# Layout of the on-chip pools at the change from FFN layer one to layer two: order of the pools, a ring of three row tiles, inner rows in the 2 KB ring

## The chip, the cores and the metric

The kernel runs on one core of a Trainium2 chip. Its engines work side by side, each through its own list of instructions in order: TensorE (PE: matmuls, with their weight loads as PEld), VectorE (DVE), ScalarE (ACT), GpSimd (POOL) and SyncE (SP), which issues nearly all DMA transfers here. They meet through semaphores. The metric is the device time in microseconds; lower is better. Data lies in HBM, in the on-chip SBUF (128 partitions; sizes below are bytes of one partition) and, for sums of matmuls, in PSUM banks.

## The reference, cut to what matters

One decoder block in float32: a mixing layer (pooling and stick-breaking attention), then a feed-forward layer, then a norm. The sequence has 2048 rows, the model width is 1024, the hidden width of the feed-forward layer is 4096.

```python
def reference(x, norm1_g, w_in, pool_w, pool_scale, pool_out_g, attn_out_g,
              w_out, norm2_g, w_up, w_down, final_g):
    B, S, _ = x.shape
    h = x
    for _ in range(DEPTH):
        hn = rmsnorm(h, norm1_g)
        proj = jnp.einsum('bsd,de->bse', hn, w_in)
        ...
        h = h + jnp.einsum('bse,ed->bsd', mixed, w_out)
        hn2 = rmsnorm(h, norm2_g)
        up = jnp.einsum('bsd,df->bsf', hn2, w_up)
        act = jnp.square(jax.nn.relu(up))
        h = h + jnp.einsum('bsf,fd->bsd', act, w_down)
    return rmsnorm(h, final_g)
```

The change concerns `up` (layer one of the feed-forward part), `act`, and the start of the product with `w_down` (layer two).

## The kernel before

**Arithmetic.** A float32 operand is split into two fp32r parts, high (ScalarE, L146) and low (VectorE, L147: operand minus high part). A product of two operands is three matmuls: high by high, high by low, low by high. Both layers are computed as a product of 2 x 2 blocks in Winograd's form, with seven products P1 to P7 in place of eight, of sums and differences of the blocks: for each half q of the sequence (1024 rows), A11, A12, A21, A22 are the blocks of the left operand (two halves of these rows by two halves of the inner width), S1 to S4 their sums.

**Layer one, `up()`.** `su` in HBM holds the row operands of layer one. For q = 0, then q = 1, the seven left operands are loaded through the ring `srp` (tiles `sr` of 4 KB, 4 slots, L929), split into `sa` (one pool of two tiles for each of the seven products: sap0 for P1, sap1 for P2, sap2 for P6, sap3 for P5, sap4 for P7, sap5 for P4, sap6 for P3) and kept for all 16 columns of that half. For a column m, 1 MB of `w_up` comes into `rb` (pool `rba` or `rbb`), its sums go to `rt` (pool `rtp`), and each product's weights are split into a tile `hw` of the pool `hlp`. A product is twelve matmuls of 128 x 512 (L1051) into a bank pX, pY or pZ; the products of one column follow each other as P2, P6, P5, P7, then P1 of the next column, P4, P3. After a product, `post()` takes the bank: ScalarE copies it (`p1`, `u2`, `u3`; L988), VectorE adds banks and copies (L996, L1004, L1020), ScalarE applies relu and square (L982, L983), and VectorE makes the sums s1, s2, s4 that layer two needs (L1011, L1014, L1016, L1024). These tiles have 2 KB each and come from the ring `avp` (11 slots); SP stores them to `sd` in HBM (L977).

**Inner sums.** For q = 1, columns come in pairs (m, m + 8). For A12 and A22 layer two uses a second level of the same form, and its row sums are made here, in the second column of each pair: `inner_rows(m)` loads two rows of q = 0 back from `sd` into one tile `hr` of 4 KB out of the ring `srp` for A22 and one for A12, both when P1 of the column is done (L870); `inner_sums` makes j1, j2 (from `avp`) and two sums in place in `hr` (L882 to L888), and stores the four to `sdi` (L880).

**Layer two, `down()`.** Steps of P1 (then P6, P7, ...): weights `wr` from `w_down` (L1120, pool `rt`) are split into `wd` (pool `t8`), rows `ar` from `sd` (L1170, pool `rs`) into `ad` (pool `s8`), and 24 matmuls for each q follow (L1391). For P1 a second `wr` is subtracted from the first (`minus`, L1124) and stored to `td` (L1126) for later use. `res` (L1195) are residual rows.

**What sets the order.** The kernel's source sets what is done; a scheduler orders the instructions of each engine when the program is built, knowing the pools and which memory comes free when. Pools are placed one behind another in the order in which they are opened, from the lowest free address. Those of layer two are opened after those of layer one have been closed, so they lie over them, and with `reuse_waits="tile"` a tile waits for exactly the earlier tiles that it overlaps. Where the pools of the two layers lie (first byte to end, in KB from the first byte of the stack that both share):

```
layer one: rtp 0-8, hlp 8-32, rba 32-40, srp 40-56 (four tiles of 4), sap0 to sap3 from 56 (16 each),
           sap6, pup, rbb, avp (11 of 2), sap4, sap5
layer two: rlp 0-16, tmp2 16-35, rs 35-55 (five of 4), rt 55-79 (six of 4), t8 (three of 8), s8 (five of 8),
           pup (eight of 8), rsp
```

So the first `rs` tiles lie over `rba` and `srp`, and the first `rt` tile over the last kilobyte of `srp` and over sap0. The last of the four `srp` slots holds the last `hr` tile.

All loads and stores named here go through SP in its one order, with at most eight on their way at a time: each new one takes one of eight semaphores in turn, and waits for the transfer that had it before.

Of the kernel before, what the change touches and what calls it, by code (L numbers as in the profile page):

```python
# [8 lines left out]
F32 = mybir.dt.float32  # L9
# [4 lines left out]
ALU = mybir.AluOpType  # L14

P = 128
S = 2048
D = 1024
T = 512
# [14 lines left out]
NEG = -1.0e30  # L34
RATIO_FRONT = (0.3, 0.4, 0.15, 0.4, 0.4, 0.3)
RATIO_TAIL = 0.6
SR = 4
LB = 4
UA = 4
LA = 5  # L40
DA = 2
# [5 lines left out]
def hymba_block(ctx: ExitStack, tc: tile.TileContext, xT, gains, w_in, pool_w, w_out, w_up, w_down, out):  # L47
    nc = tc.nc
    PS = bass.MemoryType.PSUM
# [86 lines left out]
    sd = [[[dram.tile([P, 2, T], F32, name=f"sd{q}_{i}_{c}") for c in range(8)] for i in range(7)] for q in range(2)]  # L136
# [701 lines left out]
    A11, A12, A22, S1, S2, S3, S4 = range(7)  # L838
# [19 lines left out]
    def up(pools, more):  # L858

        saps, hlp, rba, rtp, srp = pools  # L860
        NM = NF // 2
        cols = [(q, m + x * (NM // 2)) for q in range(2) for m in range(NM // 2) for x in range(2)]
        halves = {}

        def inner_rows(m):

            for i in (A22, A12):
                halves[i, 0] = r = srp.tile([P, 2, T], F32, tag="sr", name="hr")
                for x in range(2):
                    at = m + x * (NM // 2)  # L870
                    nc.sync.dma_start(r[:, x], sd[0][i][at // 2][:, at % 2])

        def inner_sums(m, i, t):

            if m < NM // 2:
                halves[i, 1] = t
                return
            a, r = halves.pop((i, 1)), halves.pop((i, 0))
            m -= NM // 2
            keep = lambda n, v: nc.sync.dma_start(sdi[i][n][m // 2][:, m % 2], v)  # L880
            s1, s2 = (avp.tile([P, T], F32, tag="av", name=n) for n in ("j1", "j2"))
            nc.vector.tensor_tensor(s1, a, t, ALU.add)  # L882
            keep(0, s1)
            nc.vector.tensor_tensor(s2, s1, r[:, 0], ALU.subtract)
            keep(1, s2)
            nc.vector.tensor_tensor(r[:, 0], r[:, 0], a, ALU.subtract)
            keep(2, r[:, 0])
            nc.vector.tensor_tensor(r[:, 1], r[:, 1], s2, ALU.subtract)  # L888
            keep(3, r[:, 1])

        what = {"P1": (A11, (0, 0), "Y", True, False), "P2": (A12, (0, 1), "X", True, True),
                "P6": (S2, (1, 1), "Y", False, False), "P5": (S1, (1, 0), "Z", True, False),
# [9 lines left out]
        raw, sums, ops, left_ops, ps, keep = {}, {}, {}, {}, {}, {}  # L902
# [67 lines left out]
        def post(q, m, s):  # L970
            k = keep.setdefault((q, m), {})
            x, y, z = (ps.get((q, m, b)) for b in "XYZ")
            new = lambda name: avp.tile([P, T], F32, tag="av", name=name)

            def put(i, t):
                if q == 0 or m >= NM // 2 or i not in (A12, A22):
                    nc.sync.dma_start(sd[q][i][m // 2][:, m % 2], t)  # L977
                if q and i in (A12, A22):
                    inner_sums(m, i, t)

            def act_of(i, src, t):
                nc.scalar.activation(t, src, AF.Relu)  # L982
                nc.scalar.activation(t, t, AF.Square)  # L983
                k[i] = t

            def copy(name):
                k[name] = pup.tile([P, T], F32, tag=name, name=name)
                nc.scalar.activation(k[name], y, AF.Copy)  # L988

            if s == "P1":  # L990
                copy("p1")
                if q and m >= NM // 2:
                    inner_rows(m - NM // 2)
            elif s == "P2":
                t = new("a11")
                nc.vector.tensor_tensor(t, x, k["p1"], ALU.add)  # L996
                act_of(A11, t, t)
                put(A11, t)
            elif s == "P6":
                copy("u2")  # L1000
            elif s == "P7":
                copy("u3")
                t = new("a22")
                nc.vector.tensor_tensor(t, z, k["u3"], ALU.add)  # L1004
                act_of(A22, t, t)
                put(A22, t)
            elif s == "P4":
                t = new("a21")
                act_of("A21", y, t)
                k[S1] = new("s1")  # L1010
                nc.vector.tensor_tensor(k[S1], t, k[A22], ALU.add)  # L1011
                put(S1, k[S1])
                k[S2] = new("s2")
                nc.vector.tensor_tensor(k[S2], k[S1], k[A11], ALU.subtract)  # L1014
                put(S2, k[S2])
                nc.vector.tensor_tensor(t, k[A11], t, ALU.subtract)  # L1016
                put(S3, t)
            elif s == "P3":
                t = new("a12")
                nc.vector.tensor_tensor(t, z, k["u2"], ALU.add)  # L1020
                act_of(A12, t, t)
                put(A12, t)
                s4 = new("s4")
                nc.vector.tensor_tensor(s4, t, k[S2], ALU.subtract)  # L1024
                put(S4, s4)
# [10 lines left out]
        rbb, pup, avp, psu = more()  # L1036
        load(*cols[1])
        lefts = [(g, q, s) for g, (q, m, s) in enumerate(slots) if m == 0 and not (q == 0 and s in order[:LB])]
        for g, (q, m, s) in enumerate(slots):
            while lefts and lefts[0][0] <= g + LA:  # L1040
                make_left(*lefts.pop(0)[1:])
            if q == 0 and 2 <= m < 6 and s in SUMS:
                sums_second(m - 2, SUMS.index(s))
            bank, first, last = what[s][2:]
            if first:
                ps[q, m, bank] = psu.tile([P, T], F32, tag=bank, name="p" + bank)
            t, w = ps[q, m, bank], ops.pop(g)
            for c in range(G):
                a = left_ops[q, s][c // 2]
                for x, (wx, ax) in enumerate(((0, 0), (0, 1), (1, 0))):  # L1050
                    nc.tensor.matmul(t, w[:, wx, c], a[:, ax, c % 2], start=first and c == 0 and x == 0,  # L1051
                                     stop=last and c == G - 1 and x == 2, skip_group_check=True)
            post(q, m, s)
            if g == 1:
                root_last(1, sslast, psu, "R")
            elif g in (6, 10):
                pr, i = psu.tile([P, T], F32, tag="R", name="pr"), g // 10
                spread(pr, yrlast[:, i])
                nc.scalar.activation(rlast[:, i], pr, AF.Copy)
            if g + UA < len(slots):  # L1060
                make_weights(g + UA)
                q2, m2, s2 = slots[g + UA]
                n = cols.index((q2, m2)) + 2
                if s2 == "P3" and n < 2 * NM:
                    load(*cols[n])

    def down(pools):
        t8, s8, rs, rt, pup, rsp, rlp, tmp_, psb = pools

        SPLIT = {"P4": A22, "P2": A12}  # L1070
        order = (("P1", A11), ("P6", S2), ("P7", S3), ("P4", A22), ("P5", S1), ("P2", A12))
# [109 lines left out]
        V = {}  # L1181
# [5 lines left out]

        def val(name, q):
            if (name, q) not in V:
                V[name, q] = pup.tile([P, 4, T], F32, tag="val", name=name)  # L1190
            return V[name, q]

        def add_residual(t, j, half, n):
# [231 lines left out]
    def catch_up(n):  # L1425
        for _ in range(n):
            with ExitStack() as behind:
                for ins in (last_split[0], done[0]):
                    if ins:
                        behind.enter_context(tc.issue_after(ins.ins))  # L1430
                later.pop(0)()
# [23 lines left out]
    def begin_ffn():  # L1455

        catch_up(len(later))
        for scope in (last_scope, out_scope, left_scope):
            scope.close()
        spool = lambda name, bufs, **kw: left_scope.enter_context(tc.tile_pool(name=name, bufs=bufs, reuse_waits="tile", **kw))  # L1460
        sap = {}
        rtp, hlp, rba, srp = (spool(n, b) for n, b in (("rtp", 1), ("hlp", UA + 2), ("rba", 1), ("srp", SR)))
        for i in range(LB):
            sap[i] = spool(f"sap{i}", 2)

        def more():
            sap[6], pup, rbb, avp = spool("sap6", 2), spool("pup", 2), spool("rbb", 1), spool("avp", 11)
            sap[4], sap[5] = (spool(f"sap{s}", 2) for s in (4, 5))
            return rbb, pup, avp, spool("psu", 2, space=PS)

        layer.append(up([sap, hlp, rba, rtp, srp], more))
        next(layer[0])

    def ffn():
        catch_up(len(later))
        front_scope.close()
        for _ in layer.pop():
            pass
        left_scope.close()
        with ExitStack() as scope:  # L1480
            spool = lambda name, bufs, **kw: scope.enter_context(tc.tile_pool(name=name, bufs=bufs, reuse_waits="tile", **kw))

            rlp, tmp2, rs, rt, t8 = spool("rlp", 2), spool("tmp2", 2), spool("rs", 5), spool("rt", 6), spool("t8", DA + 1)
            s8, pup, rsp = spool("s8", 2 * DA + 1), spool("pup", 8), spool("rsp", 2)
            down([t8, s8, rs, rt, pup, rsp, rlp, tmp2, spool("psb", 1, space=PS)])

    x0_scope = inner.enter_context(ExitStack())

# [19 lines left out]
    tail(True)  # L1508
    run()
    ffn()  # L1510


# [60 lines left out]
```

## Time and profile before

| what | value |
|---|---|
| median of 3 runs (1943.66, 1947.26, 1946.0) | 1946.0 us |
| the profiled execution, its own time | 1947.62 us |
| its span in the profile | 1945.7 us |
| mean granted TensorE clock | 0.991 |
| layer one, q = 1, and the turn to layer two | about 980 to 1328 us |

How to read what follows. The page and the views of the trace name an engine, a line of the kernel (L1051), what is written and read by the program's names (`pY<-sa,hw`), a count (x12) and times in microseconds. `SPq` is a transfer at the time of its issue by SP, `DMA` in the chain the transfer from issue to landing. In the view of waits a row names who waited, for whom, then the total, how often, and the longest. In the timeline a row is start, length, what, and in brackets how long the engine stood idle before it and what ended that. In windows a row is the stretch, its length, the busy time and count of TensorE's instructions where it is asked for TensorE (left out where it isn't), the granted clock (1.00 is full), the DMA engines' mean busy share (the packets' time can overlap to just over 1) and GB/s. In the list of DMA issues a row ends with KB and the median time from issue to landing.

### The profile page before, as it was taken

To read this page: it belongs to the slowest core of one execution; us is meant where nothing else is said; L and a number is where in the kernel's file an instruction comes from. 1 tells how busy PE (TensorE), PEld (TensorE's weight loads), DVE (VectorE), ACT (ScalarE), POOL (GpSimd) and SP (SyncE) were. 2 spreads that over 40 slices of the span, in tenths; PEclk is the share of its full clock that TensorE was granted. 3 is DMA by queue.
4 is the path that set the end of the run, shared out by engine and by line. 5 is a ranking of instruction groups with operands and counts; after the bars stand their busy time and mean duration, and the time that the engine had idled before them with its cause. 6 is when DMAs were issued, how large, how long until landed. Compare 5 with 4: busy or idle time off the path is not lost.

```text
span 1945.7 us, 26308 instructions
## 1 busy us (share of the span) xinstructions
PE 1905.2 (98%) x9043; PEld 1589.0 (82%) x9043; DVE 1384.6 (71%) x2026; ACT 994.7 (51%) x1580; POOL 206.3 (11%) x399
## 2 busy tenths in 40 slices
PE   9999999999999999999999999997999999999997
PEld 7888888887888888888878888875888888887887
DVE  6887799667876975777586777665565548649874
ACT  5565576455544555455575555553333255424643
POOL 0212123102111110000000000000020020006120
PEclk9999999999999999999999999998999999999999
DMA  6685787898696954677486666549898859957852
GB/s 222 205 271 178 232 273 215 253 325 272 235 381 231 336 188 145 221 245 251 171 265 220 222 217 239 203 166 388 301 343 303 293 203 317 335 191 267 320 205 89
DMA packets 197359, 483.44 MB, mean 248 GB/s; under 512 B 22496, under 2 KB 42976, under 8 KB 193120
## 3 DMA queue, kind: packets, MB, share of 16 engines
q1 hardware_dynamic: 197072, 481.40, 71.7%
q8 instruction: 73, 1.20, 0.3%
q14 instruction: 70, 0.57, 0.1%
q10 hardware_dynamic: 144, 0.26, 0.0%
HBM read 320.10 MB, written 161.48 MB: 248 GB/s over the span
## 4 chain that ended last, share of the span: by engine, by line
PE 72%; DVE 3%; DMA 1%; issue 1%; ACT 0%; POOL 0%; SPq 0%; DVEq 0%; ACTq 0%
PE pb L1391 21%; PE pY L1051 18%; PE pZ L1051 9%; PE pb L1229 7%; PE pX L1051 4%; PE pd L177 4%; PE pd L175 3%; PE pd L176 3%; PE pb L1334 1%; PE pr L228 1%; DVE ad L147 0%; DVE u L1200 0%; DMA sr<-su 0%; PE pm L202 0%; PE po L672 0%
## 5 line engine op out<-in xcount | busy, mean ns | idle before, releaser
L1391 PE MATMUL pb<-ad,wd 128*128 128x512 f32 x1872 | 429.6, 391 | 16.1 <-ACT ad L146 16.1
L1391 PEld LDWEIGHTS pb<-ad,wd 128*128 128x128 f32 x1872 | 352.6, 189 | 89.6 <-ACT ad L146 16.5
L1051 PE MATMUL pY<-sa,hw 128*128 128x512 f32 x1536 | 366.0, 390 | 2.5 <-ACT u L988 2.5
L1051 PEld LDWEIGHTS pY<-sa,hw 128*128 128x128 f32 x1536 | 289.0, 188 | 63.4 <-ACT u L988 3.3
L175 PE MATMUL pd<-h,hl 128*128 128x512 f32 x752 | 299.6, 398 | 0.7 <-DVE qkr L421 0.7
L177 PE MATMUL pd<-h,hl 128*128 128x512 f32 x752 | 296.9, 395 | 0.0
L176 PE MATMUL pd<-h,hl 128*128 128x512 f32 x752 | 296.4, 394 | 0.0
L147 DVE TENSOR_TENSOR ad<-ar,ad 128x1024 fp32r<-128x1024 f32 x136 | 175.6, 1300 | 50.5 <-ACT ad L146 50.2
L146 ACT ACTIVATE ad<-ar 128x1024 fp32r<-128x1024 f32 x136 | 142.5, 1051 | 115.3 <-PE pb L1391 69.1
L1051 PE MATMUL pZ<-sa,hw 128*128 128x512 f32 x768 | 184.9, 389 | 0.0
L1051 PEld LDWEIGHTS pZ<-sa,hw 128*128 128x128 f32 x768 | 144.4, 188 | 29.9
L175 PEld LDWEIGHTS pd<-h,hl 128*128 128x128 f32 x752 | 142.1, 189 | 28.2 <-DVE qkr L421 1.0
L177 PEld LDWEIGHTS pd<-h,hl 128*128 128x128 f32 x752 | 141.7, 188 | 27.8
L176 PEld LDWEIGHTS pd<-h,hl 128*128 128x128 f32 x752 | 141.9, 189 | 27.0
L146 ACT ACTIVATE hl<-raw 128x512 fp32r<-128x512 f32 x168 | 103.9, 630 | 107.1 <-PE pd L177 69.4
L1229 PE MATMUL pb<-ad,wd 128*128 128x512 f32 x672 | 154.3, 390 | 3.4 <-DVE ad L147 3.4
L1229 PEld LDWEIGHTS pb<-ad,wd 128*128 128x128 f32 x672 | 125.6, 188 | 31.8 <-DVE ad L147 5.9
L147 DVE TENSOR_TENSOR hl<-raw,hl 128x512 fp32r<-128x512 f32 x168 | 114.6, 687 | 51.1 <-ACT hl L146 48.1
L147 DVE TENSOR_TENSOR hw<-rt,hw 128x512 fp32r<-128x512 f32 x128 | 87.6, 687 | 72.8 <-ACT hw L146 72.7
L146 ACT ACTIVATE wd<-wr 128x1024 fp32r<-128x1024 f32 x48 | 50.9, 1060 | 147.4 <-PE pb L1391 111.6
L147 DVE TENSOR_TENSOR wd<-wr,wd 128x1024 fp32r<-128x1024 f32 x48 | 58.8, 1224 | 67.6 <-ACT wd L146 67.3
L1051 PE MATMUL pX<-sa,hw 128*128 128x512 f32 x384 | 93.0, 389 | 0.0
(213 smaller groups left out, 2628.5 us busy)
## 6 DMA issues: line engine op xcount, KB each, us to landing
ar<-sd SPq DMA_DIRECT2D x104, 512.0 KB, 5.6
rb<-in_w_up_dram SPq DMA_DIRECT2D x32, 1024.0 KB, 6.0
wr<-in_w_down_dram SPq DMA_DIRECT2D x64, 512.0 KB, 5.6
sd<-a SPq DMA_DIRECT2D x112, 256.0 KB, 3.4
raw<-in_w_in_dram SPq DMA_DIRECT2D x50, 512.0 KB, 4.9
sd<-s SPq DMA_DIRECT2D x96, 256.0 KB, 3.4
raw<-in_w_out_dram SPq DMA_DIRECT2D x32, 512.0 KB, 5.5
ar<-sdi SPq DMA_DIRECT2D x32, 512.0 KB, 5.1
```

The lines of the kernel that those rows point to most:

```text
L146: nc.scalar.activation(hi, src, AF.Copy)
L147: return nc.vector.tensor_tensor(lo, src, hi.bitcast(F32), ALU.subtract)
L175: nc.tensor.matmul(ps, hl[:, 0, c], hi, start=(k == 0), stop=False)
L176: nc.tensor.matmul(ps, hl[:, 0, c], lo, start=False, stop=False)
L177: mm = nc.tensor.matmul(ps, hl[:, 1, c], hi, start=False, stop=(k == n - 1))
L228: mm = nc.tensor.matmul(pr[:, b * P:(b + 1) * P], yr[:, x, b:b + 1].to_broadcast([P, P]), identr, start=(b == 0 and x == 0), stop=(b == TB ...
L1051: nc.tensor.matmul(t, w[:, wx, c], a[:, ax, c % 2], start=first and c == 0 and x == 0, stop=last and c == G - 1 and x == 2, skip_group_che ...
L1229: nc.tensor.matmul(b, t[:, wx, 2 * (kk % 2) + c, i * P:(i + 1) * P], a[:, ax, c], start=p in ("P1", "P5", "P2") and kk == 0 and c == 0 and ...
L1334: nc.tensor.matmul(b[:, cols], t[:, wx, c, n * P:(n + 1) * P], a[:, ax, c, cols], start=False, stop=(i == 1 and c == 1 and x == 2), skip_g ...
L1391: nc.tensor.matmul(ps[q, n], t[:, wx, c, n * P:(n + 1) * P], left_[q][:, ax, c], start=(n_ in ("P1", "P5", "P3") and kk == 0 and c == 0 an ...
```

## The change

Four things are done. The ring `srp` gets three slots. `hr` rows come from the ring `avp` instead, as two tiles of 2 KB each, and `avp` gets 13 slots; the rows for A22 are loaded after P1 as before, those for A12 after P2. The pools of layer two are opened in another order, with `pup` cut into `pupa` (two tiles, for the values of P1) and `pup` (six). The size of all is the same in both layers.

```diff
-SR = 4
+SR = 3
...
-        def inner_rows(m):
-
-            for i in (A22, A12):
-                halves[i, 0] = r = srp.tile([P, 2, T], F32, tag="sr", name="hr")
-                for x in range(2):
-                    at = m + x * (NM // 2)
-                    nc.sync.dma_start(r[:, x], sd[0][i][at // 2][:, at % 2])
+        def inner_rows(m, i):
+
+            halves[i, 0] = r = [avp.tile([P, T], F32, tag="av", name="hr") for _ in range(2)]
+            for x in range(2):
+                at = m + x * (NM // 2)
+                nc.sync.dma_start(r[x], sd[0][i][at // 2][:, at % 2])
...
             if s == "P1":
                 copy("p1")
                 if q and m >= NM // 2:
-                    inner_rows(m - NM // 2)
+                    inner_rows(m - NM // 2, A22)
             elif s == "P2":
+                if q and m >= NM // 2:
+                    inner_rows(m - NM // 2, A12)
                 t = new("a11")
...
-                V[name, q] = pup.tile([P, 4, T], F32, tag="val", name=name)
+                V[name, q] = (pupa if name == "p1" else pup).tile([P, 4, T], F32, tag="val", name=name)
...
-            sap[6], pup, rbb, avp = spool("sap6", 2), spool("pup", 2), spool("rbb", 1), spool("avp", 11)
+            sap[6], pup, rbb, avp = spool("sap6", 2), spool("pup", 2), spool("rbb", 1), spool("avp", 13)
...
-            rlp, tmp2, rs, rt, t8 = spool("rlp", 2), spool("tmp2", 2), spool("rs", 5), spool("rt", 6), spool("t8", DA + 1)
-            s8, pup, rsp = spool("s8", 2 * DA + 1), spool("pup", 8), spool("rsp", 2)
-            down([t8, s8, rs, rt, pup, rsp, rlp, tmp2, spool("psb", 1, space=PS)])
+            rlp, pupa, rs, rt, t8 = spool("rlp", 2), spool("pupa", 2), spool("rs", 5), spool("rt", 6), spool("t8", DA + 1)
+            s8, tmp2, pup, rsp = spool("s8", 2 * DA + 1), spool("tmp2", 2), spool("pup", 6), spool("rsp", 2)
+            down([t8, s8, rs, rt, pupa, pup, rsp, rlp, tmp2, spool("psb", 1, space=PS)])
```

The uses of `r[:, x]` in `inner_sums` become `r[x]`. After this `srp` ends at 52 KB, the `sap` pools begin there, and in layer two `rs` lies at 32 to 52 KB (over the end of `hlp`, `rba` and most of `srp`), `rt` at 52 to 76 KB over the last `sr` slot's end, sap0 and sap1, `t8` and `s8` over the pools of P2, P6, P5 and P3. The first tile of `rs` begins 64 bytes before the end of `hlp`, and the last tile there is the `hw` of the last product.

Since memory comes free at other times, the scheduler sets other orders. SP before, at the end of layer one: the last sums of a21 and a12 are stored, then the last inner sums (`sdi`), then layer two's first loads (`wr`, then `ar` of both sequence halves).

```order
L977 DMA sd_5_7_416<-a_13267 128x512
L977 DMA sd_1_7_384<-a_13290 128x512
L880 DMA sdi_0_3_428<-j_13295 128x512
L880 DMA sdi_1_3_432<-j_13296 128x512
L977 DMA sd_6_7_424<-s_13305 128x512
L880 DMA sdi_2_3_436<-hr 128x512
L880 DMA sdi_3_3_440<-hr 128x512
L1120 DMA wr<-in_w_down_dram 128x1024
L1170 DMA ar<-sd_0_0_313 128x1024
L1170 DMA ar<-sd_0_0_369 128x1024
L1120 DMA wr<-in_w_down_dram 128x1024 x2
```

All of layer one's stores stand ahead of the first load of layer two. SP in the changed kernel, first from the last column's start:

```order
L870 DMA hr<-sd_2_3_332 128x512
L870 DMA hr<-sd_2_7_336 128x512
L1121 DMA wr<-in_w_down_dram 128x1024 x6
L976 DMA sd_3_3_396<-s_13154 128x512
L976 DMA sd_4_3_404<-s_13157 128x512
L976 DMA sd_5_3_412<-a_13151 128x512
L870 DMA hr<-sd_1_3_324 128x512
L870 DMA hr<-sd_1_7_328 128x512
L976 DMA sd_6_3_420<-s_13181 128x512
L976 DMA sd_0_7_376<-a_13204 128x512
```

Six loads of layer two's weights have moved ahead of the stores of the last but one column. Directly behind these rows the order goes on, up to the first row loads of layer two:

```order
L1127 DMA td_0_473<-wr 128x1024
L1121 DMA wr<-in_w_down_dram 128x1024
L1127 DMA td_1_474<-wr 128x1024
L1121 DMA wr<-in_w_down_dram 128x1024 x2
L1196 DMA res<-hs_281 128x512
L1127 DMA td_2_475<-wr 128x1024
L976 DMA sd_2_7_392<-a_13256 128x512
L879 DMA sdi_0_3_444<-j_13261 128x512
L1121 DMA wr<-in_w_down_dram 128x1024
L879 DMA sdi_1_3_448<-j_13262 128x512
L879 DMA sdi_2_3_452<-hr 128x512
L1171 DMA ar<-sd_0_0_313 128x1024
```

The first `ar` has moved ahead of the stores that come from the last product's post-work, and three `td` stores and four more `wr` loads have moved ahead of it. ScalarE before, over the same stretch (a12 of the last but one column, a11 and a22 of the last, and so on):

```order
L988 ACTIVATE u_13208<-pY 128x512
L982 ACTIVATE a_13165<-a_13165 128x512
L983 ACTIVATE a_13165<-a_13165 128x512
L982 ACTIVATE a_13188<-a_13188 128x512
L983 ACTIVATE a_13188<-a_13188 128x512
L988 ACTIVATE u_13238<-pY 128x512
L982 ACTIVATE a_13240<-a_13240 128x512
```

and now:

```order
L981 ACTIVATE a_13177<-a_13177 128x512
L982 ACTIVATE a_13177<-a_13177 128x512
L987 ACTIVATE u_13224<-pY 128x512
L146 ACTIVATE wd<-wr 128x1024 x3
L981 ACTIVATE a_13204<-a_13204 128x512
L982 ACTIVATE a_13204<-a_13204 128x512
L987 ACTIVATE u_13254<-pY 128x512
L981 ACTIVATE a_13256<-a_13256 128x512
```

Three splits of layer two's weights have moved between the copy `u2` (u_13208 before, u_13224 now) and the copy `u3` (u_13238, u_13254) of the last column, and the last but one column's a12 ahead of `u2`. Lines of the changed kernel are one lower up to L990 and one higher from there on.

More of the change, by code (lines that the diff above doesn't have):

```diff
@@ L883, in inner_sums @@
             keep(0, s1)
-            nc.vector.tensor_tensor(s2, s1, r[:, 0], ALU.subtract)
+            nc.vector.tensor_tensor(s2, s1, r[0], ALU.subtract)
             keep(1, s2)
[L886 to L889, printed above, removed]
+            nc.vector.tensor_tensor(r[0], r[0], a, ALU.subtract)
+            keep(2, r[0])
+            nc.vector.tensor_tensor(r[1], r[1], s2, ALU.subtract)
+            keep(3, r[1])
         what = {"P1": (A11, (0, 0), "Y", True, False), "P2": (A12, (0, 1), "X", True, True),
@@ L1067, in down @@
     def down(pools):
-        t8, s8, rs, rt, pup, rsp, rlp, tmp_, psb = pools
+        t8, s8, rs, rt, pupa, pup, rsp, rlp, tmp_, psb = pools
         SPLIT = {"P4": A22, "P2": A12}
```

## The prediction

> **What bounds the kernel now.** I read the page's busy times first, then TensorE's waits, then the chain of waits around the two places where the diff acts, then the timeline there.
>
> ```profile
> span 1945.7 us, 26308 instructions
> PE 1905.2 (98%) x9043; PEld 1589.0 (82%) x9043; DVE 1384.6 (71%) x2026; ACT 994.7 (51%) x1580; POOL 206.3 (11%) x399
> PE pb L1391 <- ACT ad L146: 16.1, 1, 16.1
> PE pY L1051 <- ACT u L988: 2.5, 2, 1.8
> ```
>
> TensorE is the bound: 98% busy, the other engines 71% or less. The change keeps the number of its instructions, so it can only fill TensorE's holes or open new ones. Of its waits for the other engines (the last two rows: total, times, longest) one of 16.1 us stands out. It is at L1391, the first matmul of FFN layer two, for the high part (`ad`) of that layer's first rows. The chain shows what was late:
>
> ```profile
> 1302.43 2.73 PE pY L1051 x12
> 1317.90 3.78 DMA sdi<-hr
> 1322.12 4.44 DMA ar<-sd
> 1327.69 263.85 PE pb L1391 x1152
> ```
>
> From the top (start, length, what): a product of layer one, the store of the last inner sums out of `hr`, and only when this has landed, at 1317.90 + 3.78 = 1321.68, the load of layer two's first rows. TensorE then runs 263.85 us without a break, so what is won before 1327.69 is kept. The engines' timeline has the rest:
>
> ```profile
> 1302.92 0.68 DVE L996 TENSOR_TENSOR a<-pX,p 128x512 f32<-128x512 f32 x1
> 1305.84 3.01 PE L1051 MATMUL pY<-sa,hw 128*128 128x512 f32 x12 [0.69 <-ACT u L988]
> 1308.69 2.88 PE L1051 MATMUL pZ<-sa,hw 128*128 128x512 f32 x12
> 1317.05 0.69 DVE L888 TENSOR_TENSOR hr<-hr,j 128x512 f32<-128x512 f32 x1
> 1321.74 0.33 SPq L1120 DMA_DIRECT2D wr<-in_w_down_dram  x1
> 1322.12 0.90 SPq L1170 DMA_DIRECT2D ar<-sd  x2
> 1326.39 1.23 DVE L147 TENSOR_TENSOR wd<-wr,wd 128x1024 fp32r<-128x1024 f32 x1 [8.65 <-ACT wd L146]
> 1326.58 1.06 ACT L146 ACTIVATE ad<-ar 128x1024 fp32r<-128x1024 f32 x1 [0.23 <-DMA ar<-sd]
> 1330.17 1.22 DVE L1124 TENSOR_TENSOR wr<-wr 128x1024 f32<-128x1024 f32 x1
> ```
>
> Layer one's last matmul ends at 1308.69 + 2.88 = 1311.57. The post-work runs on to 1317.74, its store lands at 1321.68, weights (1321.74) and rows (1322.12) are issued at once, and the split (1326.58, 1.06 us) lets TensorE go at 1327.69.
>
> **The change part by part.** *What it removes.* Before, the pools of the first weights `wr` and of the first rows `ar` lie where the inner rows `hr` lay, so both loads wait for the last `hr` store. In the new layout `hr` is in another ring. The first `wr` tiles lie over operands of P1 and P2 of the layer, read for the last time some products earlier, and six of these loads are issued there. The first `ar` tile still overlaps one 64-byte strip of the weights (`hw`) of the last product, and waits for 1311.57 alone. The wait for 1321.68 is gone.
>
> *The most it can give.* An `ar` issued at 1311.6 that lands as fast as a load on an idle queue (the median from issue to landing of the first `wr` load, next fence, first row: 3.5 us) is there at 1315.1; with 1.06 us of split TensorE starts at 1316.2, a gain of 1327.69 − 1316.2 = 11.5 us.
>
> *What it puts ahead.* SP issues all transfers in its own order, and in the new order there stand between the first subtraction's store (`td`) and the first `ar`: three `td` stores and four `wr` loads of 512 KB, and `res`, `sd` and three `sdi` of 256 KB. What a busy queue costs:
>
> ```profile
> wr<-in_w_down_dram SPq DMA_DIRECT2D x1, 512.0 KB, 3.5
> sd<-a SPq DMA_DIRECT2D x1, 256.0 KB, 2.0
> 1315.00:1317.00 2.00, 0.70 1.05 404
> ar<-sd SPq DMA_DIRECT2D x4, 512.0 KB, 9.3
> ```
>
> The first two are a load at 1321.7 and a store at 1305 with nothing before them; the third is a window of two microseconds in which the engines are full (share 1.05) at 404 GB/s; the fourth are loads issued from 1324 to 1330, behind others. At 404 GB/s 512 KB take 1.30 us and 256 KB 0.65 us, so the short store has 2.0 − 0.65 = 1.35 us besides its bytes. Ahead of `ar` are 7 × 1.30 + 5 × 0.65 = 12.3 us of bytes. They begin when the first `td` is made: two `wd` (1.23 us each) and a subtraction (1.22 us) on DVE, 3.7 us. DVE takes them up right behind the sum that ended at 1302.92 + 0.68 = 1303.60, or up to 2 us earlier, since the new order has TensorE finish the preceding column's P4 and P3 before P6 instead of in the midst of it. So bytes flow from 1305.3 to 1307.3, `ar` lands between 1305.3 + 12.3 + 1.30 + 1.35 = 1320.2 and 1322.2; middle 1321.2. With 1.06 us TensorE starts at 1322.3: gain 1327.69 − 1322.3 = **5.4 us**. The DVE steps that the new order still has ahead of the low part of `ar` end some 1.8 us later than the 1317.74 of before (one 1.22 us subtraction and half a microsecond of waiting moved in between), at 1319.5, and are hidden.
>
> On this the rule of the Trainium skill, "DMA: Bandwidth & Descriptors", section "Queues, rings and completion order", can be laid: each DMA engine takes its descriptors in ring order, while completion is not first in, first out. The 9.3 us against 3.5 us above agree with the first half, which makes `ar` wait for the bytes ahead; if instead rows could pass them, TensorE would start soon after the 1316.2 of the cap, which is the first rival.
>
> *ACT.* The three `wd` splits, 3 × 1.06 = 3.2 us, now stand in ACT's order ahead of the relu of a11 and of the copy `u3`, and `u3` releases the bank for P4's matmuls (the row at 1305.84, [0.69 <-ACT u L988]). If ACT comes to them by about 1300.6, they end by 1303.8 and `u3` is as early as before: 0. If only at 1302.3, where ACT's squaring before the row at 1302.92 ended, relu and square follow to 1306.8 and `u3` to 1307.4, 1.6 us later, and P3 waits as much for the sum `a22` behind it. Between 0 and −1.7 I take **−0.4**, since the new PE order makes the earlier case the likelier.
>
> *The clock.* After the hole TensorE's granted clock is low:
>
> ```profile
> 1327.60:1331.00 3.40, 3.31 (x8) 0.50 1.03 419
> 1331.00:1334.00 3.00, 3.00 (x11) 0.69 1.02 407
> ```
>
> That costs 3.40 × 0.50 + 3.00 × 0.31 = 2.6 us. The hole is still 1322.3 − 1311.6 = 10.7 us, and the clock had fallen within 5.4 us (the window from 1315 to 1317 has a mean of 0.70), so nothing of it is won or lost: 0.
>
> *Three `sr` slots in place of four.* At the turn from the first half of the sequence to the second all left operands are loaded anew through this ring:
>
> ```profile
> 994.32 8.04 DMA sr<-su
> 1002.44 1.06 ACT L146 ACTIVATE sa<-sr 128x1024 fp32r<-128x1024 f32 x1 [5.50 <-DMA sr<-su]
> 1003.40 0.58 ACT L988 ACTIVATE u<-pY 128x512 f32<-128x512 f32 x1
> 1004.03 4.54 PE pY L1051 x12
> ```
>
> ACT stands at the split of a late `sr`, the copy `u` behind it waits, and TensorE 1.8 us for that (the second wait above). With three slots a load is issued when the tile three before it, not four, is split: later by at most one tile's pair of splits, 1.06 + 1.23 = 2.3 us. The load that is late is then another one in the same place. Between a gain of 1.8 and a loss of 2.3 I take 0, as what makes it late is the 8.04 us in a queue with a load of weights, which stays. At layer one's start the same three slots fill while other work of ScalarE and DVE goes on: 0, the same 2.3 us at worst.
>
> *The inner rows in the ring of 2 KB tiles.* Eight columns of the second half load `hr` from the 13-slot ring (11 before). A pair of columns claims 14 values and 4 sums, 18, and now 4 rows more, 22. A pair is fourteen products of 2.72 us, 38.1 us (the 2.73 us of the chain's row are one of them), so a slot comes round again after 11/18 × 38.1 = 23.3 us before and 13/22 × 38.1 = 22.5 us now.
>
> ```profile
> sd<-a SPq DMA_DIRECT2D x41, 256.0 KB, 2.2
> sdi<-hr SPq DMA_DIRECT2D x28, 256.0 KB, 3.2
> hr<-sd SPq DMA_DIRECT2D x24, 256.0 KB, 3.2
> ```
>
> A row tile lives longest: loaded (3.2 us), kept from P1 to the sum after P7, about 4.5 products = 12 us, stored (3.2 us): some 16 us, the load within the 12. Slack some 6 us: 0 here; the price without it is the third rival. Everything behind the restart keeps its order by layer, with weights further ahead than before: 0.
>
> Sum: 5.4 − 0.4 = **5.0 us**. The profiled execution took 1947.62 us, 1.9 more than its span, and would take 1942.6; it lies 1.6 above the median of the runs, 1946.0, which gives **1941 us**.
>
> **The rivals.** *The rows come early.* The four `wr` and three `td` are spread over DVE's pace and the queue is not full when `ar` is issued. For it: the engines were almost idle when the six weights are now to come, so these should be in by 1300:
>
> ```profile
> 1290.00:1300.00 10.00, 1.00 0.03 9
> ```
>
> (share 0.03, 9 GB/s). Against it: from 1315 the window of 404 GB/s shows them full with less to move. `ar` lands about 1317, TensorE starts at 1318: gain 9.5, time about 1936.5.
>
> *The hole only changes its cause.* The queue's line before `ar` is as long as that of the 9.3 us row: an `ar` issued at 1314.5, behind a `wr` whose slot has to come free, lands at 1323.8 and TensorE starts at 1324.9; ACT's −1.7 comes on top. Gain 2.8 down to 1.1, time 1943 to 1945, no change that can be told. For it: three `td` stores stand ahead of `ar` that before came after it.
>
> *Slower: the ring of 13.* If a row's slot isn't free when a column's value is to be written, ACT stands at the relu, with `u2` and `u3` queued behind it, and TensorE waits for these at the banks. The eight pairs would each pay this. It decides from (5.0 + 3.9)/8 = 1.1 us a pair; at 2 us a pair the time is 1946 − 5 + 16 = 1957. For it: ring position counts per claim and the second column of a pair claims 15 of the 22. Against: in the whole of layer one TensorE waited twice, 2.5 us, none of it in these columns but 0.69, and the slack is about 6 us.
>
> **How the numbers follow.** About 0.2%, 3.9 us, is what a measurement of this kernel can tell from no change. The forecast (gains of 3 to 7.5) has 0.55, and 0.07 of it lies under 3.9; the early rows 0.14; the changed cause 0.20; the slow ring, or a longer turn at 1000 us by the same standing ACT, 0.11. Faster: 0.48 + 0.14 = 0.62. Same: 0.07 + 0.20 and 0.01 of the slow ring, 0.28. Slower: 0.10. The forecast's own range is 1938.5 to 1943; the range for 8 in 10 takes in the early rows, almost to the cap (1946.0 − 11 = 1935), the changed cause and the small loss of 1 us, up to 1947.
>
> **What would show it.** In the changed profile the wait at the first L1392 matmul should be near 10.7 us in place of 16.1; the chain should run from the last product or an L1127/L1121 transfer to `ar<-sd`, with no `sdi<-hr` before it; `ar` should show some 7 us from issue to landing. Six `wr` loads should land before 1300, and P3 should start within half a microsecond of its place. An `ar` of 4 us says early rows, of 9 us or more the changed cause. Waits of L1052 for ACT copies or DVE sums in the columns after 1020 us, where there is 0.69 now, say slow ring. The prediction fails if layer one's matmuls no longer end by about 1312, or if layer two's first stretch breaks up into several pieces of the chain.

## The result, and the profile after

The change takes 1941.2 us (median of 8 runs, 1937.44 to 1944.16) against 1945.66 us before (8 runs beside it, 1943.28 to 1948.71): ratio 0.9975, 95% interval 0.9963 to 0.9986. A second set of runs (E5) gave 0.9972 (0.9962 to 0.9981). So it is faster by 4.5 to 5 us, a quarter of a percent; 1941 us was forecast.

The page of the changed kernel, the head:

```profile
span 1937.1 us, 26281 instructions
```

TensorE's waits in it (total, times, longest):

```profile
PE pb L1392 <- ACT ad L146: 12.5, 1, 12.5
PE pY L1052 <- ACT u L987: 1.2, 2, 0.7
```

and its chain at the turn to layer two (start, length, what):

```profile
1304.19 7.74 DMA wr<-in_w_down_dram
1312.00 6.92 DMA ar<-sd
```

The wait at layer two's first matmul is 12.5 us where it was 16.1. No `sdi<-hr` stands before `ar` in the chain any more; in its place stands a load of weights. It was issued at 1304.19 and landed at 1311.93; `ar`, which takes over the same one of SP's eight semaphores, went out at 1312.00. The timeline of the same stretch:

```profile
1301.04 0.34 SPq L1127 DMA_DIRECT2D td<-wr  x1
1301.79 3.02 PE L1052 MATMUL pY<-sa,hw 128*128 128x512 f32 x12 [0.69 <-ACT u L987]
1304.64 2.88 PE L1052 MATMUL pZ<-sa,hw 128*128 128x512 f32 x12
1312.00 0.32 SPq L1171 DMA_DIRECT2D ar<-sd  x1
1318.94 1.06 ACT L146 ACTIVATE ad<-ar 128x1024 fp32r<-128x1024 f32 x1 [7.10 <-DMA ar<-sd]
```

The last product ends at 1304.64 + 2.88 = 1307.52, `ar` is issued 4.48 us later and lands at 1318.92. The late issue alone does not make the landing late: the `sdi` store ahead of it, issued at 1310.07, lands 7.7 us after that, near 1317.8, and `ar` only about 1.1 us behind it. ScalarE splits it at once, and TensorE starts at 1320.05.

The span is 8.6 us shorter than that of before, and that is not all the change. The profiles differ by some microseconds upstream of layer two: the last product starts at 1308.69 before and at 1304.64 here, and in the kernel of E1, whose order at the turn is that of before, at 1303.33. From that start to the end of the span it is 1945.7 − 1308.69 = 637.0 us before, 1937.1 − 1304.64 = 632.5 here: 4.5 us less, the same as the medians. I compare kernels by this stretch, and by the piece of it up to layer two's first matmul: 19.00 us before (1327.69 − 1308.69), 15.41 here (1320.05 − 1304.64). After that matmul it is 618.0 and 617.1 us; E1's 618.8 shows that kernels with one order at the turn differ by as much.

### The profile page after: what moved, and what is told of

It reads as the page before. It is cut to its first block, busy times and chain, and to the rows that moved or that the text cites. A ratio compares the mean times of both kernels' runs of the same rounds, so it can differ in the third digit from the quotient of the medians.

```text
span 1937.1 us, 26281 instructions
## 1 busy us (share of the span) xinstructions
PE 1902.7 (98%) x9043; PEld 1588.3 (82%) x9043; DVE 1383.2 (71%) x2026; ACT 991.2 (51%) x1580; POOL 210.2 (11%) x399
## 4 chain that ended last, share of the span: by engine, by line
PE 84%; issue 8%; DVE 4%; DMA 2%; POOL 1%; ACT 1%; SPq 0%; DVEq 0%; ACTq 0%; POOLq 0%
PE pY L1052 17%; PE pb L1392 17%; PE pZ L1052 8%; PE pd L175 8%; PE pd L177 8%; PE pd L176 8%; PE pX L1052 4%; PE pb L1230 2%; PE po L672 2%; PE pta L661 1%; PE pr L228 1%; PE pz L614 1%; PE pm L202 1%; DMA res<-hs 1%; PE pz L615 1%
## 5 line engine op out<-in xcount | busy, mean ns | idle before, releaser
L1392 PE MATMUL pb<-ad,wd 128*128 128x512 f32 x1872 | 429.8, 392 | 12.5 <-ACT ad L146 12.5
L1052 PE MATMUL pY<-sa,hw 128*128 128x512 f32 x1536 | 364.3, 390 | 1.2 <-ACT u L987 1.2
L1052 PEld LDWEIGHTS pY<-sa,hw 128*128 128x128 f32 x1536 | 288.2, 188 | 61.6 <-ACT u L987 2.0
L1052 PE MATMUL pZ<-sa,hw 128*128 128x512 f32 x768 | 184.7, 390 | 0.0
L1052 PEld LDWEIGHTS pZ<-sa,hw 128*128 128x128 f32 x768 | 144.2, 188 | 29.8
L1052 PE MATMUL pX<-sa,hw 128*128 128x512 f32 x384 | 93.1, 390 | 0.0
```

The source lines that it names most:

```text
L1392: nc.tensor.matmul(ps[q, n], t[:, wx, c, n * P:(n + 1) * P], left_[q][:, ax, c], start=(n_ in ("P1", "P5", "P3") and kk == 0 and c == 0 an ...
```

## The experiments

**E1, the pools' order alone; E2, three `sr` slots and 13 in the 2 KB ring, and no more.** Two parts of the change. E1 has layer two's new pool order, with `hr` still in four `sr` slots; to the kernel before it does

```diff
-            rlp, tmp2, rs, rt, t8 = spool("rlp", 2), spool("tmp2", 2), spool("rs", 5), spool("rt", 6), spool("t8", DA + 1)
-            s8, pup, rsp = spool("s8", 2 * DA + 1), spool("pup", 8), spool("rsp", 2)
+            rlp, pupa, rs, rt, t8 = spool("rlp", 2), spool("pupa", 2), spool("rs", 5), spool("rt", 6), spool("t8", DA + 1)
+            s8, tmp2, pup, rsp = spool("s8", 2 * DA + 1), spool("tmp2", 2), spool("pup", 6), spool("rsp", 2)
```

and the matching choice of `pupa` in `val`. E2 is the kernel before with

```diff
-SR = 4
+SR = 3
...
-            sap[6], pup, rbb, avp = spool("sap6", 2), spool("pup", 2), spool("rbb", 1), spool("avp", 11)
+            sap[6], pup, rbb, avp = spool("sap6", 2), spool("pup", 2), spool("rbb", 1), spool("avp", 13)
```

> The kernel before with layer two's pools in the changed order, and nothing else: four sr slots, inner rows in that ring. Theory A (the gain comes from the hole at the turn to layer two, and from there because the inner rows left the memory of the first loads): the first wr tile now lies over the last sr slot with the last inner rows, SP's order at the turn is word for word that of before, so the wait at the first L1392-like matmul stays 15.5 to 16.5 us and the time is that of before within 1 us. Theory B (the order of the pools alone frees the first loads): wait near 12.5 us, time 4 us less than before.

> The kernel before with three sr slots and 13 slots in the 2 KB ring; inner rows stay in the sr ring, layer two's pools in the old order. Theory A: the weights come early, but the first row tiles still lie over the last inner rows, so the wait at layer two's first matmul stays within 15 to 16.5 us; the turn to the second half of the sequence near 1000 us is as before; time 0 to 1 us less than before. Theory C (the three slots win 2.8 us at the turn near 1000 us, as the profile of the change shows 4.05 us of lead at the last product where it had 1.2 at 988 us): time 2 to 3 us less than before, with TensorE's wait for ACT's copies near 1000 us at 0.7 in place of 1.8 us and the first product after it in 3.1 in place of 4.5 us.

E1: ratio to before 1.0001 (0.9991 to 1.0010), wait 16.2 us. Theory A holds: without moving the inner rows the pools' order gives nothing. E2: ratio 1.0037 (1.0022 to 1.0051), slower by 6 to 7 us, which neither theory expected. E2's first row of TensorE's waits, and its chain at the turn to layer two:

```profile
PE pb L1391 <- ACT ad L146: 23.9, 1, 23.9
```

```profile
1310.06 9.61 DMA wr<-in_w_down_dram
1319.73 5.72 DMA sd<-a
1325.47 6.54 DMA ar<-sd
```

Here the weights' loads came early and the rows' did not. Weights and `td` stores went ahead of layer one's last stores, these waited behind them, and the rows behind all: the hole grew from 16.1 to 23.9 us. The landing of the last `hr` stores is not what held the first `ar`. In SP's timeline

```profile
1324.22 0.97 SPq L880 DMA_DIRECT2D sdi<-hr  x2
```

these stores land 5.7 us or more after their issue, near 1330, and `ar` goes out at 1325.47, as soon as the `sd` store of the chain has landed (1319.73 + 5.72 = 1325.45). Its place in SP's order held it. By the layout the first tile of `rs` (35 to 39 KB) lies over `rba`, and only the later ones reach the `srp` slots; why the scheduler put all the rows last is not shown.

The timeline of E2 at the turn near 1000 us, and the same product in E1:

```profile
1002.49 3.04 PE L1051 MATMUL pY<-sa,hw 128*128 128x512 f32 x12 [1.13 <-ACT u L988]
```

```profile
1000.30 3.01 PE L1051 MATMUL pY<-sa,hw 128*128 128x512 f32 x12 [1.67 <-ACT u L988]
```

The wait is 1.13 us. Over all profiles taken it is 1.7 and 1.8 with four slots and 0.5 to 2.2 with three. The product takes 3.04 us, as theory C expected, but E1 has 3.01 with four slots: the 4.54 us were of one profile. So theory C falls; at most some tenths of a microsecond come from the three slots.

**E3, the rows moved, pools in the old order; E4, the change with the strip freed.** E3 is the change with E1's diff undone: layer two's pools as they were before. E4 is

```diff
-            rlp, pupa, rs, rt, t8 = spool("rlp", 2), spool("pupa", 2), spool("rs", 5), spool("rt", 6), spool("t8", DA + 1)
+            rlp, pupa, pad = spool("rlp", 2), spool("pupa", 2), spool("pad", 1)
+            pad.tile([P, 64], F32, tag="pad", name="pad")
+            rs, rt, t8 = spool("rs", 5), spool("rt", 6), spool("t8", DA + 1)
```

> The change without the new order of layer two's pools: inner rows in the 2 KB ring, three sr slots, old order. The first rows then lie over rba and early sr slots and SP's order has five row loads and six weight loads right after the last column's start, some 20 us before layer one ends. Theory A: the hole of 12.5 us in the changed kernel is the late first rows alone (issued 4.5 us after the last product, behind the td and wr transfers); with the rows early TensorE goes on within 1.5 us and keeps its clock, which saves another 2.6 us: 14 to 18 us less than before, near 1929. Theory D (the new order of the pools is needed, since other late pools stand in the way): the wait stays above 10 us and the time near that of the change or above it.

> The change with 256 bytes left free ahead of the pool of row tiles, so that its first tile no longer overlaps the last 64 bytes of the weights of layer one's last product. Theory A: the first rows move to the last column's start in SP's order, TensorE's wait at the first matmul of layer two falls from 12.5 to 1.5 us or less and the clock stays up: 9 to 14 us less than the change, 14 to 18 less than before. Theory E (what holds the first rows is the length of the queue, not the overlap): the wait stays near 10 us and the time within 3 us of the change.

E3: 1934.32 us, ratio 0.9944 (0.9930 to 0.9958). E4: 1934.21 us, ratio 0.9943 (0.9930 to 0.9957). Both beat the change by about 6 us and the kernel before by 11 to 12, where 14 to 18 were expected of the early rows. E3 differs from E2 by the rows' move alone, and is 18 us faster: the move makes the gain. The new pool order is not needed for it, and as the change has it, it costs more than half of what moving the rows can give: 64 bytes of overlap with the last product's weights. The first `ar` of E4 is issued 20 us before the last product, but the hole does not close (timeline of E4, ScalarE and VectorE):

```profile
1284.60 0.45 SPq L1171 DMA_DIRECT2D ar<-sd  x1
1304.60 2.88 PE L1052 MATMUL pZ<-sa,hw 128*128 128x512 f32 x12
1309.92 0.68 DVE L1021 TENSOR_TENSOR a<-pZ,u 128x512 f32<-128x512 f32 x1
1310.64 0.63 ACT L981 ACTIVATE a<-a 128x512 f32<-128x512 f32 x1 [3.76 <-DVE a L1021]
1311.17 4.83 ACT L146 ACTIVATE ad<-ar 128x1024 fp32r<-128x1024 f32 x5
1312.26 5.96 PE L1392 MATMUL pb<-ad,wd 128*128 128x512 f32 x18 [4.78 <-ACT ad L146]
```

The rows have long been there. ScalarE stands 3.76 us at the relu of the last a12, which waits for VectorE's sum (1309.92), and the splits are queued behind it. So TensorE still waits 4.78 us (5.4 us in E3) where 1.5 or less was expected, and the clock did not stay up. In E4's window behind the hole (stretch, length, TensorE, clock, share, GB/s) the clock is 0.57, and 4.00 × 0.43 = 1.7 us are lost:

```profile
1312.00:1316.00 4.00, 3.74 (x9) 0.57 1.05 412
```

**E5 and E6, the change again, and with a ring of 11**, which is

```diff
-            sap[6], pup, rbb, avp = spool("sap6", 2), spool("pup", 2), spool("rbb", 1), spool("avp", 13)
+            sap[6], pup, rbb, avp = spool("sap6", 2), spool("pup", 2), spool("rbb", 1), spool("avp", 11)
+            spool("pad", 1).tile([P, 1024], F32, tag="pad", name="pad")
```

> The change itself, a second profile and more times beside the next three on one chip. If the hole's reduction is the gain, the stretch from the start of layer one's last product to layer two's first matmul is again 15.4 us within 0.5 (19.0 before), with ar issued when the wr load eight transfers ahead of it has landed; the lead of 1 to 3 us that the first profile shows over layer one comes and goes with the profile.

> The change with 11 in place of 13 slots in the 2 KB ring (4 KB left unused behind it, so that all else keeps its place). By the slack worked out (a slot comes round every 11/22 of 38.1 us = 19 us, a row tile lives some 16) the ring still holds: time within 2 us of the change. If the ring is what a pair of columns stands on (third rival), the eight pairs with rows lose 1 to 2 us each, 8 to 16 us more than the change, with TensorE's waits at L1052 well above 2 us.

E5's profile shows the stretch to the first matmul as 14.4 us (1320.96 − 1306.54), `ar` issued 3.48 us after the last product; the whole stretch to the end is 1938.5 − 1306.54 = 632.0 us, 5.1 less than before. That is 0.5 us outside of what was expected, on the side of a larger gain. E6: 1941.95 us, ratio 0.9975 (0.9964 to 0.9985), as the change; waits at L1052 are 2.0 us in two, at the turn near 1000 us and before P4 of the last column. So TensorE does not feel the ring, even with two slots fewer. VectorE does, once, at the turn to layer two: it stands 5.9 us ahead of a sum that goes into a ring tile (L1015), until a store out of the ring has landed; in the change, with 13 slots, one such wait was 2.0 us (L883). The rows land later still. In E6's profile the stretch to the first matmul is 16.1 us (1323.14 − 1307.04).

**E7 and E8, the splits ahead of the relu** in E3 and in E4:

```diff
-                split((left_[q][:, 0], left_[q][:, 1]), rows[q])
+                with tc.high_priority() if g == 0 else nullcontext():
+                    split((left_[q][:, 0], left_[q][:, 1]), rows[q])
```

> E3 with the splits of layer two's first two row tiles ahead of the relu of the last a12 in ScalarE's order, nothing else moved. If the hole of 5.4 us that E3 kept is ScalarE standing at that relu (which waits for VectorE's sum) with the loaded rows behind it, the first matmul follows the last product within 1.5 us, then waits for the low part behind the same sum on VectorE: 1 to 3 us less than E3. If it is the late wr that the chain of E3 names, nothing changes.

> E4 with the same two splits moved ahead of the relu. As for E3 and E7: 1 to 3 us less than E4 if ScalarE's order makes the rest of the hole, nothing if the weights do.

E7: 1932.33 us, ratio 0.9936 (0.9920 to 0.9951). E8: 1932.65 us, ratio 0.9928 (0.9912 to 0.9945). By the medians that is 2.0 and 1.6 us less than E3 and E4, by the ratios 1.6 and 2.9; the intervals overlap, so it is the timeline of E8 that shows the effect:

```profile
1307.52 1.04 ACT L146 ACTIVATE ad<-ar 128x1024 fp32r<-128x1024 f32 x1
1308.61 1.19 PE L1393 MATMUL pb<-ad,wd 128*128 128x512 f32 x4 [0.64 <-ACT ad L146]
1311.06 1.06 ACT L146 ACTIVATE ad<-ar 128x1024 fp32r<-128x1024 f32 x1 [2.50 <-DVE a L1021]
1312.17 14.15 PE L1393 MATMUL pb<-ad,wd 128*128 128x512 f32 x54 [2.36 <-ACT ad L146]
```

The first four matmuls follow the last product after 0.64 us; then TensorE stands 2.36 us more, for the second split, which waits for the same sum of VectorE, as the theory has it. The hole is 3.0 us in place of 4.8, and in E7 3.7 in two waits in place of 5.4. From the last product's start to the end of the span E8 takes 625.4 us against 627.3 in E4, but E7 626.3 against 625.7 in E3. So the shorter hole is shown, and that the time falls by as much is not.

**E9, the change with its `td` stores held back; E10 and E11, the same in E8 and E7** (here the first three subtractions come behind VectorE's last inner sum). E9 is

```diff
-                split((left_[q][:, 0], left_[q][:, 1]), rows[q])
+                lo = split((left_[q][:, 0], left_[q][:, 1]), rows[q])
             if extra is not None:
-                minus(blk(b12 if n == "P1" else b21, kk), extra, 1 if n == "P1" else 2, kk)
+                b = blk(b12 if n == "P1" else b21, kk)
+                with tc.issue_after(lo.ins) if g < 3 else nullcontext():
+                    minus(b, extra, 1 if n == "P1" else 2, kk)
```

> The change with the subtractions of layer two's first three weight blocks (and so their td stores and the next wr loads behind them) held until the low parts of the rows are made; the first ar keeps its wait for the last product. If the three td and four wr ahead of ar hold it (the queue term of the prediction), ar is issued within 1 us of the last product's end instead of 3.5 to 4.5 after it and lands in 4 to 5 in place of 6.9 us: hole near 6.5 in place of 11.5 to 12.5 us, time 5 to 6 us less than the change. If the queue is not what holds it, hole and time stay.

> E8 with the first three subtractions behind layer one's last sum on VectorE. The low part of the first rows and a12's sum come some 2.4 us earlier on VectorE (two subtractions of 1.22 us less ahead), so the second wait at layer two's start falls from 2.4 us to 1 us or less: 1 to 2.5 us less than E8. Against it: td stores and weights come later, and layer two's later steps may wait for weights; then TensorE waits anew after the first three steps and the time is not less.

> E7 with the same three subtractions behind layer one's last sum: as for E10, 1 to 2.5 us less than E7, or no less if later steps wait for weights.

E9: 1937.73 us, ratio 0.9962 (0.9948 to 0.9975), 2 to 3.5 us less than the change (by the ratios and by the medians) where 5 to 6 were expected. Its timeline:

```profile
1303.58 2.88 PE L1052 MATMUL pZ<-sa,hw 128*128 128x512 f32 x12
1307.18 1.30 SPq L1171 DMA_DIRECT2D ar<-sd  x1
1313.99 1.06 ACT L146 ACTIVATE ad<-ar 128x1024 fp32r<-128x1024 f32 x1 [4.63 <-DMA ar<-sd]
1315.10 11.20 PE L1394 MATMUL pb<-ad,wd 128*128 128x512 f32 x37 [8.64 <-ACT ad L146]
```

`ar` goes out 0.72 us after the last product's end (1306.46): the queue's line was what held its issue. But it still takes 6.8 us to land, behind layer one's own stores. E10: 1930.96 us, ratio 0.9922 (0.9908 to 0.9935). E11: 1932.30 us, ratio 0.9925 (0.9911 to 0.9938). The second wait fell from 2.36 to 1.6 us in E10, where 1 us or less was expected, and the times can't be told from E8 and E7. The stretch from the last product's start to the end of the span hints at a gain, 623.8 us against 625.4 in E8 and 622.3 against 626.3 in E7, from one profile each. Later steps did not wait for weights.

The fastest of these is E10, 1930.96 us: the rows' memory freed, the first splits ahead of the relu, the early subtractions late. Its lead on E8 and E11 is within the intervals; its lead on both kernels of this study is not.

## Why the prediction was right, point by point

**The bound and the place.** Right. The gain sits between the start of layer one's last product and layer two's first matmul: 3.6 of the 4.5 us in the first profile, 4.6 of the 5.1 in the second. E1 shows that the pools' order does nothing while the inner rows lie where they lay, and E3 against E2 that moving them does it. One detail is not as I had it: I said that both first loads wait for the last `hr` store. SP waits for it ahead of `wr`, and `ar` stands behind `wr` in its order; E2 shows an `ar` that goes out before that store has landed.

**The first rows' wait (5.4 us forecast, 3.6 and 4.6 measured, and 2.9 in E6, which has the same loads and stores at the turn).** The mechanism was right, with one term mis-sized: the rate of the queue. I took 404 GB/s. The windows of the change from the first `td` store to about the issue of `ar` (stretch, length, clock, share, GB/s):

```profile
1300.00:1304.00 4.00, 1.00 0.84 292
1304.00:1308.00 4.00, 1.00 1.03 350
1308.00:1312.00 4.00, 0.98 0.99 328
```

and the same stretch of E5:

```profile
1302.90:1313.00 10.10, 0.93 0.98 328
```

At nearly full share the engines moved 328 to 350 GB/s. The 7 x 524,288 + 5 x 262,144 bytes ahead of `ar`, 4.98 MB, take 15.1 us at 330 GB/s in place of 12.3; with `ar` itself and latency, 2.65 us by the prediction, 17.7 us, and from 1301.04 to the landing at 1318.92 it is 17.9. That the two agree so well is in part luck, for the mean rate over this whole stretch is higher:

```profile
1301.04:1318.92 17.88, 0.80 1.01 363
```

At 363 GB/s the engines moved 6.5 MB in it, 1.0 MB more than `ar` and what I had counted ahead of it. The stores and `hr` rows issued before 1301.04 are not in my sum, nor what passes of the transfers issued after `ar`; how the rest divides between them is open. The trace of before has a window for it, too:

```profile
1310.00:1315.00 5.00, 1.00 0.96 304
```

These are layer one's last stores, at 304 GB/s with a share of 0.96; I had taken the window behind it. The `td` store began 3.60 us ahead of the last product, about the early end of what I had given (3.4 to 1.4), which took 1.2 us of the error back. I had also counted bytes alone: E9 and the chain show that `ar` was first held at its issue, by the semaphore of the load eight transfers ahead. As it landed right behind the store ahead of it, that hold by itself cost little.

**ScalarE's splits ahead of `u3` (−0.4).** They cost nothing: P4 starts 2.85 us before the last product in both kernels (1305.84 and 1308.69; 1301.79 and 1304.64), with the same wait of 0.69 us. This 0.4 made up for some of the rate.

**The clock (0).** Right. After the hole the clock of the change is

```profile
1320.00:1324.00 4.00, 3.95 (x9) 0.50 1.04 399
1324.00:1327.00 3.00, 3.00 (x11) 0.76 1.03 412
```

4.00 × 0.50 + 3.00 × 0.24 = 2.7 us lost, against 2.6 before.

**Three slots, the ring, layer two's later course (0 each).** Right as far as these runs can tell: by the waits near 1000 us over all profiles, by E6, and by the 617.1 and 617.5 us after the first matmul (618.0 before).

**The total (5.0 us forecast, 4.5 and 5.0 measured).** That it came so close is partly luck. The wait gave less than its 5.4 us, the 0.4 us for ScalarE was not spent, and 0.9 and 0.5 us came behind the first matmul, where the forecast has nothing and where profiles differ by as much without the change.

**The rivals.** Rows did not come early: `ar` took 6.9 us to land. The hole did change its cause in part, for `ar` now waits for a weight load; E2, where weights go ahead and the rows gain nothing, shows that this can cost 7 us. The slow ring, as a cost to TensorE, is refuted for 13 and for 11 slots.

What I did not see is how much was left. I read the 64-byte strip as a wait that costs nothing, since the last product must end anyway; it decides where SP's order puts the first rows, and E4 gets some 6 us from removing it.

## What to carry to other kernels

Where two stages share memory, look for the load that the next stage needs first, and for the last thing that lies under it: an overlap of 64 bytes can set a transfer's place in a queue, and with it several microseconds. Let the loads of all that the first step needs come early together; weights alone fill the queue ahead of the rows and make it worse (E2). When the load is early, the next late thing is the order of the engine that prepares it (E4 to E8).

## What the runs showed of the hardware that was not expected

The DMA engines' share does not tell their rate: near full share they moved 328 GB/s in the change from 1308 to 1312 us (above), and in the same stretch of E4

```profile
1308.00:1312.00 4.00, 1.00 1.02 413
```

413 GB/s. `td`, `wr`, `sd` and `sdi` transfers are under way in both; what makes the difference was not tried.

A hole of three microseconds can cost clock as well. E8's two short waits, 0.64 and 2.36 us, were followed by these windows:

```profile
1310.00:1312.00 2.00, 0.00 (x0) 1.00 1.02 410
1312.00:1316.00 4.00, 3.83 (x12) 0.70 1.04 410
1316.00:1319.00 3.00, 3.00 (x13) 0.83 1.03 412
```

The granted clock is 1.00 through the hole and falls behind it; 4.00 × 0.30 + 3.00 × 0.17 = 1.7 us are lost there, after a hole that was itself only 0.64 + 2.36 = 3.0 us. E4's 4.78 us cost the same 1.7 us.
